# Convolved units of a delta-net mixer summed in one region of a PSUM bank, with due work bound in order

## The chip, the core and the metric

The kernel runs on one core of one Trainium2 chip. The metric is the device time of one execution in microseconds, where lower is better. A core has TensorE (matmuls, PE in the profile, its weight loads PEld), VectorE (DVE), ScalarE (ACT), GpSimd (POOL) and SyncE (SP), which issues most DMAs. Matmuls write to PSUM, which has eight banks of 128 partitions by 512 fp32 values; VectorE and ScalarE read it from there.

## What is computed

A decoder trunk of two layers over 256 tokens of width 1024. Each layer is a half SwiGLU feed-forward block, a token mixer, cross-attention into 256 memory tokens, and a second half feed-forward block. Layer 0 mixes by dilated window attention beside a gated linear recurrence; layer 1 by a gated delta net, whose q, k and v go through a causal convolution of four taps. Cut to the layers' frame and the second mixer:

```python
for layer in range(DEPTH):                                   # 2
    x = x + 0.5 * swiglu(rmsnorm(x, ffn1_norm[layer]), ffn1_w_in[layer], ffn1_w_out[layer])
    h = rmsnorm(x, mix_norm[layer])
    x = x + (attn_lru_mixer(h, ...) if layer % 2 == 0 else deltanet_mixer(h, ...))
    x = x + cross_attention(rmsnorm(x, xa_norm[layer]), rmsnorm(mem, xa_mem_norm[layer]), ...)
    x = x + 0.5 * swiglu(rmsnorm(x, ffn2_norm[layer]), ffn2_w_in[layer], ffn2_w_out[layer])
return rmsnorm(x, final_norm)

def deltanet_mixer(h, w_in, conv_w, a_log, dt_bias, o_norm, w_out):   # 8 heads of 128
    qkv, z, a, b = jnp.split(h @ w_in, [3 * W, 4 * W, 4 * W + DN_HEADS], axis=-1)
    qkv = jax.nn.silu(causal_dwconv(qkv, conv_w))
    q, k, v = jnp.split(qkv, 3, axis=-1)
    q, k = l2norm(q.reshape(shp)), l2norm(k.reshape(shp))
    beta = jax.nn.sigmoid(b)
    g = -jnp.exp(a_log) * jax.nn.softplus(a + dt_bias)
    o = gated_delta_rule_chunked(q, k, v, g, beta)
    o = rmsnorm(o, o_norm) * jax.nn.silu(z)
    return o.reshape(B, S, W) @ w_out
```

## The kernel before

Activations lie transposed: 128 partitions of features by 256 tokens, eight such pieces for the width of 1024. To keep fp32 accuracy with the fast fp32r products, every operand is split into a rounded high part and the rest, the low part. A weight tile of 512 rows by 256 columns comes by DMA (`raw`, five buffers), ScalarE writes its high part (L158) and VectorE its low part (L159) into `wt` (four buffers).

A *unit* is 1024 rows by 256 columns of one weight matrix: two halves `j` of 128 output features, each over eight steps `k`. The generator `unit` takes one bank of PSUM for each half. In `mm3` a step is two products: the high weights times the moving high and low part side by side (512 columns, L200) and the low weights times the high part (256 columns, L204). The bank then holds two regions whose sum is the result; `add` copies one on ScalarE (L270) and adds the other on VectorE (L271). `unit_t` is the same with tokens and features exchanged (L216, L220). `parts` (L242) makes three products of 256 columns that all sum in one region; `unit_split` uses it, both halves in one bank, and reads that bank once at the end.

A unit yields after every four steps, four times in all. At each yield the driver (`run` or `fill`) calls `tick`, which splits one weight tile ahead, runs one piece of `later`, counts time up by one and runs the *due* work: `after(n, fn)` notes work that is to be issued n ticks on. The second mixer is written as units in a given order (`DN_ORDER`) with everything else as due work: betas, decays, the decay rows that go out to DRAM and come back by GpSimd's DMA (`decay`, L1119, exponentials L1125), norms (`sums`), transposes, the key matrices, the block inverses. Two groups of two head pairs then run a back substitution (`back`, twelve yields), alternately, and after each yield as many pieces of the next units as `DN_FILL` says; its last two numbers stand ahead of the transposes of the gated output (`gated_T`, L1348 to L1350) of the second group, and what is left of the units runs after them, ahead of the output projection.

The units of q, k and v in the second mixer (`unit` within `mixer1`) hand each half to `conv`: the addition into `xn`, a scaled copy by tap 3 on ScalarE (L1071) and three multiply-adds with the other taps on VectorE (L1074, 72 in all: 24 halves). psw, the pool that the units of this mixer take banks from, has three banks; the small products use pss (three) and psf (two).

The order written in the program is not the order of issue. A scheduler at compile time keeps each engine's instructions in one fixed queue, and takes those first that it believes ready first; equal ones go in the program's order. The engines then work through their queues in order and wait on semaphores.

In the first mixer the heads run in a loop of ten rounds: scores of head h (`scores`), probabilities transposed for h - 1 (`weights`, L658), values for h - 2 (`values`, L892 to L894), then two pieces of other units.

## Time and profile before

| | us |
|---|---|
| median of three runs | 1252.77 |
| lowest and highest run | 1252.73, 1253.04 |
| the profiled execution | 1251.99 |
| its span (first to last instruction) | 1250.2 |
| TensorE busy | 1236.0 (99%) |
| VectorE busy | 929.0 (74%) |
| ScalarE busy | 752.0 (60%) |
| first mixer's attention rounds, from and to | about 252, 296 |
| second mixer's units, from and to | about 784, 949 |
| granted clock of TensorE | 0.998 |

All rows come from one profiled execution of the kernel. Times are from the start of its span. Matmuls overlap each other, and their ends are modelled, so the busy share of TensorE says little; what a product costs is read from its start to the next one's start. "idle" in a row is the time that the engine stood still just before, and the arrow names what ended it.

### The profile page before, as it was taken

The page shows a single profiled execution, that of the slowest core. Times are in us where ns is not written, and L with a number is a line of the kernel's source. Part 1 is how long each engine was busy: PE and PEld are TensorE (multiplying, and loading weights), DVE is VectorE, ACT ScalarE, POOL GpSimd, SP SyncE. Part 2 cuts the span into 40 slices and gives each one's busy share as a digit, 9 for nine tenths or more (in the row PEclk, how much of TensorE's full clock was granted, in tenths as well). Part 3 has the DMA queues.
Part 4 walks back from the last instruction along what each step waited for, and adds up shares of the span by engine and source line. Part 5 has one row for each costly group of instructions (what it writes and reads, how often), then busy time and mean ns, then how long its engine had stood idle before and what let it go on. Part 6 is the DMA issues. An engine that isn't in the chain of part 4 may idle for free.

```text
span 1250.2 us, 20300 instructions
## 1 busy us (share of the span) xinstructions
PE 1236.0 (99%) x7702; PEld 1104.9 (88%) x7702; DVE 929.0 (74%) x1590; ACT 752.0 (60%) x1281; POOL 80.5 (6%) x96
## 2 busy tenths in 40 slices
PE   9999999999999999999999999999999999999997
PEld 8888889888998888888888888888898998888887
DVE  6987957788668778766877756989757668777753
ACT  7766545886555665545656544776757465666543
POOL 1000020000101000011000001020001101000000
PEclk9999999999999999999999999999999999999999
DMA  8766676544544566557666566667534535666561
GB/s 272 215 206 197 185 255 185 178 125 152 185 135 154 185 198 184 183 185 231 187 187 195 181 192 204 183 153 193 142 99 135 181 124 169 185 186 194 177 194 60
DMA packets 231019, 222.92 MB, mean 178 GB/s; under 512 B 14969, under 2 KB 228617, under 8 KB 230793
## 3 DMA queue, kind: packets, MB, share of 16 engines
q1 hardware_dynamic: 229448, 217.94, 56.9%
q0 software_dynamic: 1152, 3.15, 1.0%
q8 instruction: 60, 0.98, 0.3%
q10 hardware_dynamic: 320, 0.53, 0.1%
q14 instruction: 39, 0.31, 0.1%
HBM read 215.03 MB, written 5.51 MB: 176 GB/s over the span
## 4 chain that ended last, share of the span: by engine, by line
PE 90%; DVE 5%; ACT 2%; DMA 1%; issue 1%; POOL 1%; ACTq 0%; DVEq 0%; POOLq 0%
PE psw L200 21%; PE pss L200 16%; PE psw L204 11%; PE psf L200 11%; PE pss L204 8%; PE psf L204 5%; PE psw L242 5%; PE psf L242 4%; PE pss L242 3%; PE psw L216 2%; DVE wt L159 1%; PE psw L220 1%; ACT wt L158 1%; PE pss L1268 1%; PE psf L1274 1%
## 5 line engine op out<-in xcount | busy, mean ns | idle before, releaser
L159 DVE TENSOR_TENSOR wt<-raw,wt 128x1024 fp32r<-128x1024 f32 (+1 forms) x409 | 484.9, 1191 | 202.8 <-ACT wt L158 199.6
L158 ACT ACTIVATE wt<-raw 128x1024 fp32r<-128x1024 f32 (+1 forms) x409 | 418.6, 1031 | 172.1 <-PE psw L204 59.4
L200 PE MATMUL psw<-x,wt 128*128 128x512 f32 x864 | 310.6, 396 | 2.1 <-DVE xn L271 1.8
L204 PE MATMUL psw<-x,wt 128*128 128x256 f32 x864 | 224.9, 281 | 0.5 <-DVE wt L159 0.5
L200 PE MATMUL pss<-x,wt 128*128 128x512 f32 x520 | 187.4, 393 | 0.0
L200 PEld LDWEIGHTS psw<-x,wt 128*128 128x128 f32 x864 | 160.6, 188 | 30.1 <-issue 2.1
L204 PEld LDWEIGHTS psw<-x,wt 128*128 128x128 f32 x864 | 162.4, 188 | 9.4 <-DVE wt L159 1.0
L204 PE MATMUL pss<-x,wt 128*128 128x256 f32 x520 | 134.9, 280 | 0.0
L200 PE MATMUL psf<-x,wt 128*128 128x512 f32 x352 | 127.2, 394 | 0.0
L200 PEld LDWEIGHTS pss<-x,wt 128*128 128x128 f32 x520 | 97.7, 188 | 16.9 <-ACT bc L377 0.4
L204 PEld LDWEIGHTS pss<-x,wt 128*128 128x128 f32 x520 | 97.7, 188 | 5.4
L200 PE MATMUL psw<-h,wt 128*128 128x512 f32 x264 | 94.9, 396 | 0.0
L204 PE MATMUL psf<-x,wt 128*128 128x256 f32 x352 | 91.3, 280 | 0.0
L200 PE MATMUL pss<-h,wt 128*128 128x512 f32 x242 | 87.0, 396 | 0.0
L336 POOL TENSOR_TENSOR acc<-acc,sq 128x256 f32<-128x256 f32 x49 | 43.7, 891 | 658.3 <-ACT sq L334 557.3
L200 PEld LDWEIGHTS psf<-x,wt 128*128 128x128 f32 x352 | 66.1, 188 | 11.2
L204 PE MATMUL psw<-h,wt 128*128 128x256 f32 x264 | 72.0, 280 | 0.0
L204 PEld LDWEIGHTS psf<-x,wt 128*128 128x128 f32 x352 | 66.2, 188 | 3.5
L204 PE MATMUL pss<-h,wt 128*128 128x256 f32 x242 | 66.0, 280 | 0.0
L200 PEld LDWEIGHTS psw<-h,wt 128*128 128x128 f32 x264 | 49.6, 188 | 10.8
L200 PE MATMUL psf<-h,wt 128*128 128x512 f32 x154 | 55.4, 397 | 0.0
L200 PEld LDWEIGHTS pss<-h,wt 128*128 128x128 f32 x242 | 45.5, 188 | 9.8
(377 smaller groups left out, 2109.2 us busy)
## 6 DMA issues: line engine op xcount, KB each, us to landing
raw<-in_ffn_w_in_dram SPq DMA_DIRECT2D x175, 512.0 KB, 3.6
raw<-in_ffn_w_out_dram SPq DMA_DIRECT2D x80, 512.0 KB, 3.6
raw<-in_xa_wkv_dram SPq DMA_DIRECT2D x32, 512.0 KB, 3.5
raw<-in_dn_w_in_dram SPq DMA_DIRECT2D x32, 512.0 KB, 4.6
raw<-in_ab_w_in_dram SPq DMA_DIRECT2D x20, 512.0 KB, 3.6
raw<-in_xa_wq_dram SPq DMA_DIRECT2D x16, 512.0 KB, 3.5
raw<-in_xa_wo_dram SPq DMA_DIRECT2D x16, 512.0 KB, 3.4
raw<-in_ffn_w_out_dram SPq DMA_DIRECT2D x16, 256.0 KB, 2.9
```

What stands on the lines that cost most here:

```text
L158: nc.scalar.activation(a, r, AF.Copy)
L159: nc.vector.tensor_sub(b, r, a.bitcast(F32))
L200: nc.tensor.matmul(out.rearrange("p a s -> p (a s)"), w[:, 0, cols], mov[:, k].rearrange("p a s -> p (a s)"), start=k == start, stop=k == ...
L204: nc.tensor.matmul(out[:, 0], w[:, 1, cols], mov[:, k, 0], start=False, stop=False)
L216: nc.tensor.matmul(out.rearrange("p a s -> p (a s)"), mov[:, k, 0, tok], w.rearrange("p a s -> p (a s)"), start=k == 0, stop=k == KD - 1)
L220: nc.tensor.matmul(out[:, 0], mov[:, k, 1, tok], w[:, 0], start=False, stop=False)
L242: self.nc.tensor.matmul(out, a[u], b[w], start=first and i == 0, stop=last and i == 2)
L336: (eng or nc.gpsimd).tensor_add(self.acc, self.acc, sq)
L1268: nc.tensor.matmul(py[:, i], na[:, i], tu[:, 0, i], start=True, stop=True)
L1274: nc.tensor.matmul(pp[:, i], yy[:, i], tu[:, 1, i], start=True, stop=True)
```

## The change

Three things are changed.

The twelve units of q, k and v in the second mixer go through a new generator, `unit_sum`: one bank for both halves, three products a step (`parts`) that sum up in one region of 256 columns, and `conv` gets that region itself and reads it from PSUM, four times. The addition into `xn` is gone there. (`lead` is never set.)

`Net.last` keeps the latest matmul of `mm3`, `mm3t` and `parts`, and the latest two instructions of a weight split. `behind` opens a context in which every instruction on the same engine as one of these is issued after it, in the engine's queue; nothing waits for its end. `tick` runs all due work in it, for TensorE, ScalarE and VectorE; the first mixer runs `weights` and `values` in it, for TensorE alone. There, one of the two pieces of each round moves from the end to between `scores` and `weights`.

The second row of `DN_FILL`, the counts of pieces in the second group, loses three: those after the second and the fifth yield, and one of the five ahead of the first gated transposes.

```diff
--- before.py
+++ after.py
@@ -26,7 +26,7 @@
 NEG = -1e30
 
 DN_ORDER = ('k0 k1 q0 q1 k2 v0 k3 v1 z0', '01|v3 z1 v2 q2', 'q3', '23|z2 z3 K2 K3')
-DN_FILL = ((1, 1, 1, 1, 1, 1, 1, 1, 1, 2, 2, 1), (1, 1, 1, 1, 1, 1, 1, 1, 1, 1, 1, 0, 5, 0))
+DN_FILL = ((1, 1, 1, 1, 1, 1, 1, 1, 1, 2, 2, 1), (1, 0, 1, 1, 0, 1, 1, 1, 1, 1, 1, 0, 4, 0))
 YB = 5
 EB, QB, VB = (4, 3, 3)
 TWICE = 'k0 k1 q0 q1'.split()
@@ -76,7 +76,7 @@
         self.n_load = self.n_half = self.n_take = 0
         self.later = deque()
         self.banks, self.n_bank = "w", 0
-        self.now, self.due = 0, []
+        self.now, self.due, self.last = 0, [], {}
 
 
 
@@ -155,8 +155,8 @@
         for u in range(0, n, step):
             us = slice(u, min(n, u + step))
             a, b, r = wt[:, us, 0, :cols], wt[:, us, 1, :cols], raw[:, us, :cols]
-            nc.scalar.activation(a, r, AF.Copy)
-            nc.vector.tensor_sub(b, r, a.bitcast(F32))
+            self.last["act"] = nc.scalar.activation(a, r, AF.Copy)
+            self.last["dve"] = nc.vector.tensor_sub(b, r, a.bitcast(F32))
         self.halves.setdefault(i, []).append(wt)
 
     def w(self, name, c0):
@@ -178,7 +178,15 @@
             self.later.popleft()()
         self.now += 1
         while self.due and self.due[0][0] <= self.now:
-            self.due.pop(0)[2]()
+            with self.behind():
+                self.due.pop(0)[2]()
+
+    def behind(self, engines=("pe", "act", "dve")):
+
+        stack = ExitStack()
+        for e in engines:
+            stack.enter_context(self.tc.issue_after(self.last[e].ins))
+        return stack
 
     def after(self, n, fn):
 
@@ -197,8 +205,9 @@
             w = wts[i // 4][:, i % 4]
 
             def high():
-                nc.tensor.matmul(out.rearrange("p a s -> p (a s)"), w[:, 0, cols], mov[:, k].rearrange("p a s -> p (a s)"),
-                                 start=k == start, stop=k == stop - 1)
+                self.last["pe"] = nc.tensor.matmul(out.rearrange("p a s -> p (a s)"), w[:, 0, cols],
+                                                   mov[:, k].rearrange("p a s -> p (a s)"),
+                                                   start=k == start, stop=k == stop - 1)
 
             def low():
                 nc.tensor.matmul(out[:, 0], w[:, 1, cols], mov[:, k, 0], start=False, stop=False)
@@ -213,8 +222,8 @@
             w = wts[k // 4][:, k % 4]
 
             def high():
-                nc.tensor.matmul(out.rearrange("p a s -> p (a s)"), mov[:, k, 0, tok], w.rearrange("p a s -> p (a s)"),
-                                 start=k == 0, stop=k == KD - 1)
+                self.last["pe"] = nc.tensor.matmul(out.rearrange("p a s -> p (a s)"), mov[:, k, 0, tok],
+                                                   w.rearrange("p a s -> p (a s)"), start=k == 0, stop=k == KD - 1)
 
             def low():
                 nc.tensor.matmul(out[:, 0], mov[:, k, 1, tok], w[:, 0], start=False, stop=False)
@@ -239,7 +248,7 @@
     def parts(self, out, a, b, first=True, last=True):
 
         for i, (u, w) in enumerate(((0, 0), (0, 1), (1, 0))):
-            self.nc.tensor.matmul(out, a[u], b[w], start=first and i == 0, stop=last and i == 2)
+            self.last["pe"] = self.nc.tensor.matmul(out, a[u], b[w], start=first and i == 0, stop=last and i == 2)
 
     def unit_split(self, name, c0, mov, dst, tokens=False):
 
@@ -254,6 +263,21 @@
             if j and ks.stop == KD:
                 self.split(dst, bank)
             yield
+
+    def unit_sum(self, name, c0, mov, take, lead=False):
+
+        wts = self.w(name, c0)
+        bank = self.bank_w()
+        sums = [bank[:, 0], self.bank_w()[:, 0] if lead else bank[:, 1]]
+        for j, ks in (LEAD if lead else STEADY):
+            js = slice(j * P, j * P + P)
+            for k in ks:
+                w = wts[k // 4][:, k % 4]
+                self.parts(sums[j], [w[:, i, js] for i in range(2)], [mov[:, k, i] for i in range(2)], k == 0, k == KD - 1)
+            if ks.stop == KD:
+                take(j, sums[j])
+            if len(ks) == 4 or j:
+                yield
 
     def unit_t(self, name, c0, mov, take):
 
@@ -950,14 +974,17 @@
             for h in range(10):
                 if h < 8:
                     sc[h] = scores(h)
+                self.fill(bg, 1)
                 if 1 <= h < 9:
-                    pts[h - 1] = weights(*sc.pop(h - 1))
+                    with self.behind(("pe",)):
+                        pts[h - 1] = weights(*sc.pop(h - 1))
                 if h >= 2:
                     i = h - 2
                     if i % 2 == 0:
                         po = self.bank("s")
-                    values(i, pts.pop(i), po)
-                self.fill(bg, 2)
+                    with self.behind(("pe",)):
+                        values(i, pts.pop(i), po)
+                self.fill(bg, 1)
             self.fill(bg)
             self.flush()
             self.project_out("ab_w_out", a2, gnext)
@@ -1063,10 +1090,8 @@
 
                 return mp.tile([P, 4, P], F32, name=name, bufs=bufs)
 
-            def conv(y, j, f, ps):
-
-                x = mp.tile([P, S], F32, name="xn", bufs=2)
-                self.add(x, ps)
+            def conv(y, j, f, x):
+
                 tap = lambda i: self.dcw[:, 24 * i + f:24 * i + f + 1]
                 nc.scalar.activation(y[:, j], x, AF.Copy, scale=tap(3))
                 for i in (2, 1, 0):
@@ -1365,8 +1390,8 @@
                     return
                 a = "qkv".index(kind)
                 y = mp.tile([P, 2, S], F32, name="y", bufs=YB)
-                yield from self.unit("dn_w_in", a * 1024 + c * 256, mov,
-                                     lambda j, ps: conv(y, j, a * 8 + 2 * c + j, ps))
+                yield from self.unit_sum("dn_w_in", a * 1024 + c * 256, mov,
+                                         lambda j, x: conv(y, j, a * 8 + 2 * c + j, x))
                 twice = 2 if step in TWICE else 1
                 silu(y, twice)
                 if kind == "k":
```

## Rows read from the trace of the kernel before

**Rows 1.** The page, part 1: busy us, share of span, instructions.
```profile
PE 1236.0 (99%) x7702; PEld 1104.9 (88%) x7702; DVE 929.0 (74%) x1590; ACT 752.0 (60%) x1281; POOL 80.5 (6%) x96
```

**Rows 2.** The page, part 4: shares of the chain that ended last.
```profile
PE 90%; DVE 5%; ACT 2%; DMA 1%; issue 1%; POOL 1%; ACTq 0%; DVEq 0%; POOLq 0%
```

**Rows 3.** Busy time by stretch of the second mixer: stretch, length, engines (instructions), clock, DMA.
```profile
784.00:845.00 61.00, 58.76 (x366) 51.71 (x365) 54.78 (x154) 46.88 (x95) 9.35 (x9) 1.00 0.67 166
...
902.00:949.00 47.00, 46.57 (x343) 43.49 (x344) 27.12 (x60) 30.42 (x74) 4.20 (x4) 1.00 0.25 80
```

**Rows 4.** TensorE's timeline: start, length, engine, line, operation, out<-in, count, [idle<-releaser].
```profile
818.39 0.39 PE L200 MATMUL psw<-x,wt 128*128 128x512 f32 x1
820.62 0.47 PE L200 MATMUL psw<-x,wt 128*128 128x512 f32 x1 [1.84 <-DVE xn L271]
...
843.75 0.47 PE L216 MATMUL psw<-wt,x 128*128 128x512 f32 x1 [0.40 <-DVE tm L1233]
...
845.70 0.50 PE L216 MATMUL psw<-wt,x 128*128 128x512 f32 x1 [0.29 <-DVE xn L271]
...
900.76 0.68 PE L1348 MATMUL pss<-ident,qk 128*128 128x128 f32 x3
902.43 0.33 PE L1348 MATMUL pss<-ident,qk 128*128 128x128 f32 x1 [1.00 <-DVE qk L1339]
...
951.97 0.28 PE L204 MATMUL psw<-a,wt 128*128 128x256 f32 x1
953.60 0.50 PE L200 MATMUL psf<-a,wt 128*128 128x512 f32 x1 [1.34 <-DVE a L1350]
```

**Rows 5.** TensorE's timeline in the first mixer.
```profile
290.31 0.98 PE L242 MATMUL psw<-m,wt 128*128 128x256 f32 x7
292.00 0.30 PE L658 MATMUL pss<-ident,pe 128*128 128x128 f32 x1 [0.70 <-DVE pe L656]
```

**Rows 6.** TensorE's timeline: the two forms of a step.
```profile
821.05 0.40 PE L200 MATMUL psw<-x,wt 128*128 128x512 f32 x1
...
821.75 0.39 PE L200 MATMUL psw<-x,wt 128*128 128x512 f32 x1
...
350.94 5.87 PE L242 MATMUL psf<-x,wt 128*128 128x256 f32 x48
356.65 1.59 PE L242 MATMUL pss<-kT,qT 128*128 128x256 f32 x12
```

**Rows 7.** Groups in 784 to 845: busy us, mean ns | idle before, releasers.
```profile
L1074 DVE SCALAR_TENSOR_TENSOR y<-xn,dcw,y 128x255 f32<-128x255 f32 (+2 forms) x42 | 19.8, 474 | 1.1 <-ACT y L1071 1.1
L159 DVE TENSOR_TENSOR wt<-raw,wt 128x1024 fp32r<-128x1024 f32 x16 | 19.5, 1219 | 0.6 <-ACT wt L158 0.5
L271 DVE TENSOR_TENSOR xn<-psw,xn 128x256 f32<-128x256 f32 x15 | 6.2, 414 | 0.1
...
L1071 ACT ACTIVATE y<-xn,dcw 128x256 f32<-128x256 f32 x14 | 7.1, 504 | 1.7 <-DVE xn L271 1.6
L270 ACT ACTIVATE xn<-psw 128x256 f32<-128x256 f32 x16 | 6.0, 373 | 2.5 <-PE psw L200 2.5
```

**Rows 8.** Groups of the whole span, columns as in rows 7.
```profile
L397 DVE SCALAR_TENSOR_TENSOR xT<-psw,xT 128x256 f32<-128x256 f32 x48 | 20.1, 419 | 5.2 <-PE psw L200 4.7
...
L1268 PEld LDWEIGHTS pss<-tu,na 128*128 128x128 f32 x96 | 11.3, 191 | 0.6 <-ACT tu L1281 0.2 <-DMA tu<-d 0.2
...
L1275 DVE COPY_PREDICATED tu<-dn_m,psf 128x512 f32<-128x512 uint8 x12 | 8.6, 731 | 3.4 <-PE psf L1274 3.4
...
L1280 PEld LDWEIGHTS pss<-ident,tu 128*128 128x128 f32 x32 | 3.7, 141 | 0.5 <-DVE tu L1275 0.3
...
L1307 ACT ACTIVATE q<-pss,eg 128x128 f32<-128x128 f32 x8 | 2.5, 368 | 3.8 <-DVE vb L1304 3.8
```

**Rows 9.** Timeline of ScalarE and of GpSimd.
```profile
817.51 0.99 ACT L1125 ACTIVATE e<-e,ngc 128x128 f32<-128x128 f32 x3 [3.95 <-DMA e<-gd]
...
811.35 3.66 POOL L1119 DMA_DIRECT2D e<-gd  x4 [0.81 <-DMA gd<-gt]
```

## The prediction

> **What bounds the kernel now.** I read the page first. TensorE is busy for 99% of the span [rows 1], and 90% of the chain that ended last is TensorE's own work [rows 2]. So nothing done on another engine is worth time by itself. A change can win only where TensorE stands still, or loses by making it stand still or by giving it more to stream. I then read the windows of the second mixer: in its first stretch VectorE is busy for 54.78 of 61 us, in the last one for 27.12 of 47 [rows 3]. The reader should see that VectorE is nearly full where eight convolved units follow each other, although TensorE still sets the pace.
>
> The third view is TensorE's timeline. Matmuls overlap, so a stall is read from start to start: a product of 512 columns is followed 0.23 us later by the next, one of 256 columns 0.12 us later, a small fp32 product 0.11 us later. Going through the second mixer by that rule, five stalls above 0.25 us belong to work that the diff touches [rows 4]: 818.39 to 820.62 is 2.23 us instead of 0.23, so 2.00 lost; the rows at 843.75 and 845.70 have 0.40 and 0.29 of idle time; the four transposes of a gated output should take 900.76 + 3 x 0.11 = 901.09, but the fourth starts at 902.43, 1.34 lost; 951.97 to 953.60 loses 1.51. The first three wait for L271, the addition that frees a bank of psw (or for small work queued ahead of it on VectorE); the fourth for the gating (L1339); the fifth for the last split of a gated output (L1350), which the output projection needs. In the first mixer one transpose of probabilities waits: seven products of 0.118 from 290.31 end at 291.14, and the next starts at 292.00, 0.86 lost [rows 5]. All this is 2.69 + 1.34 + 1.51 + 0.86 = 6.40 us. That is the whole prize.
>
> **The change part by part.** *Sums in one region.* For each of 12 units with a convolution the pair "512 columns, then 256" becomes three products of 256, each with its own weight load. Columns are the same, 768. From rows [rows 6]: two steps of the old form from 821.05 to 821.75, 0.35 us each; 48 products of the new form (16 steps) from 350.94 to 356.65, 0.119 each, 0.357 a step. 12 x 16 = 192 steps x 0.007 = **+1.3 us**, on TensorE, so on the path. Ends: +0.5 to +2, since a step's start is given to 0.01. The Trainium skill, "TensorE: Matmul & The Clock Gate", section "Back-to-back issue gap", has N / 2.4 + 2.5 ns, by which a third product would cost 2.5 ns a step; an estimate by that page is 0.5 us for all 192, and the rows' 0.231 us for 512 columns is longer than its 0.216.
>
> What goes is the addition: 24 copies on ScalarE of 0.37 us (L270) and 24 additions on VectorE of 0.41 (L271), of the 15 or 16 of each in the first stretch [rows 7]. On VectorE that is 15 x 0.41 = 6.2 of its 54.78 busy us there. The three taps (L1074, 0.474 each) and the scaled copy (L1071, 0.50) stay, but read PSUM; the nearest row, a SCALAR_TENSOR_TENSOR with a PSUM operand, is 0.419 against 0.474 from SBUF [rows 7, 8]. So the taps become no dearer; 0 to -0.06 each, off the path. I book nothing for relief by itself; it counts through the stalls below.
>
> *The bank waits (2.69 us).* A unit now needs one bank where it needed two, so the three banks of psw hold three units instead of one and a half, and the addition that the stalled products waited for is gone. Against it: the 2.00 us have a second cause. ScalarE stood 3.95 us for the decay rows that come by DMA (e<-gd), loaded by GpSimd from 811.35 on, and the exponentials held its queue [rows 9]. These loads and that landing stay; the softplus chain that leads to them shares VectorE with the additions and gets faster. Binding the due exponentials behind the last split doesn't move them if that split was done long before. I take **-2.2** of the 2.69; ends 0 and -2.69.
>
> *Due work bound behind products and splits.* On TensorE due products come after the tick's last product, on ScalarE and VectorE after the last split. Queued behind a bound instruction on VectorE or ScalarE are the taps of the next unit; behind a bound product, the next products. The masks, stores and loads of SP and GpSimd are not bound; only their producers move. No row of TensorE's waits in this mixer was ended by a weight split, so later stores ahead of weight loads on SP's queue are booked at nothing; were the five raw buffers used up, each load held back would cost its own delay. The gated transposes (1.34 us) are among the bound: they come behind the products of their tick, with gating done by then. GpSimd's power ahead of them is untouched. I take **-1.1**, ends 0 and -1.34.
>
> *The fill counts.* Three of sixteen pieces of z and K go from between the back-substitution steps and from ahead of the gated transposes to after them: the projection's wait of 1.51 gets three pieces of four steps, 3 x 4 x 0.35 = 4.2 us, as cover. What is next late: two steps (the counts that became 0) lose their piece and see the predicated copy of 0.73 us (L1275, [rows 8]) uncovered unless due products stand there; I leave 0.1 for it. **-1.4**; ends -1.51 and 0 (both holes open, 2 x 0.73).
>
> *First mixer.* A piece of four steps now lies between scores and weights, and the weights' transposes come behind it, so the 0.86 us get a cover of 1.4. **-0.7**; ends 0 and -0.86.
>
> *The new wait.* Both halves of a unit now lie in one bank. The first half's convolution reads while the second half's products want to write there. Does the program let them? In the back substitution ScalarE's L1307 reads columns of a bank that VectorE's L1304 does not touch and needs none of its results, and yet waits for it, 3.8 us in all [rows 8]. So readers of one bank are held apart whatever their columns, and I expect the same for TensorE: twelve locks. The Trainium skill, "PSUM — Partial Sum Buffer", section "PSUM bank collisions raise a hardware error", says that engines must be guarded by bank and quadrant, not by address; it speaks against this change, and the row of L1307 agrees. Bare, a lock lasts as long as the scaled copy and three taps, 0.50 + 3 x 0.474 = 1.92 us [rows 7], so 12 x 1.92 = 23 us if TensorE has nothing else. It has: the next unit's first half lies in another bank and is 8 x 0.35 = 2.8 us long, and due products come first. The nearest rows are the back-substitution steps, where TensorE also waits for an evacuation of its own result with other products in between: L1268 and L1280 lost 0.6 and 0.5 us in 24 and 8 groups of four, 0.03 to 0.06 a group [rows 8]. The convolution is longer than such an evacuation, so I take 0.1 each, **+1.2**; ends 0 (a wait can't give time) and +23.
>
> **Sum.** -2.2 - 1.1 - 1.4 - 0.7 + 1.3 + 1.2 = -2.9 us. The profiled execution took 1251.99 us, 1250.2 of it the span and 1.8 around it; with the change 1249.1. The median of the three runs is 1252.77, 0.78 above the profiled one, so the forecast is 1252.77 - 2.9 = about **1249.8**.
>
> **The rivals.** *The locks stay open (slower).* Where the next unit's weights are not split in time, or the convolution queues behind a split (1.2 us, L159 [rows 7]), the cover is too short. For it speaks that VectorE is 90% busy in the first stretch; against it that 6.2 us of that go. Without locks the sum is -4.1, so it turns at 4.1 / 12 = 0.34 us a lock. At half the bare price, 0.96 each or 11.5 in all, the time is 1252.77 - 4.1 + 11.5 = 1260; at 0.7 each it is 1257. This is also what the bank rule gives as a mechanism.
>
> *One wait takes the other's place (no change).* The exponentials still hold ScalarE's queue for the DMA, so the 2.00 us stay (they may now hold a convolution and with it a lock), and locks cost 0.2: -5.4 + 2.0 + 1.3 + 2.4 = +0.3, 1253.1. For it: the DMA chain isn't touched.
>
> *All stalls go.* Locks are wholly covered: -6.40 + 1.3 = -5.1, 1247.7. For it: the due work that fills a lock is now placed there by name. Against it: 818 us has the DMA behind it.
>
> **How the numbers follow.** Forecast 0.45 (three quarters of it below the line of "faster"), all stalls go 0.20, no change 0.18, locks open 0.17. About 0.2%, 2.5 us, is what a measurement of this kernel can tell from no change; faster is below 1250.3, slower above 1255.3. Faster 0.35 + 0.20 = 0.55; same 0.10 + 0.18 = 0.28; slower 0.17. The range reaches from 1246.0 (all stalls and a little more) to 1257.0 (locks of 0.7 us) and leaves out about 0.15. The likeliest case alone spans 1248 to 1251.5.
>
> **What the changed profile would show.** L271 on xn gone but for the one of the gates; 576 more products at the line of the three-product form in place of 192 at L200 and 192 at L204; TensorE's waits in the first stretch ended by L1074 (a lock), each under 0.2 us if I'm right, near 1 if the slower rival is; the stall near 952 gone and products of K between the last gated transposes and the projection; no wait of 1 us at L1348; the transposes of the first mixer behind a piece, without the 0.86. I'm wrong if waits ended by L1074 sum to over 4 us, if ScalarE's wait for e<-gd still stops TensorE for 2 us, or if the three-product step takes over 0.36 us.

## The result and the profile after

The change made the kernel slower: a median of 1263.68 us (1262.35 to 1264.69, five runs) against 1252.77 (1252.70 to 1255.92, five runs), a ratio of 1.0079 with a 95% interval of 1.0065 to 1.0093. That is 10.9 us more where 2.9 less was forecast, and above the range. The profiled execution took 1264.2 us, 1262.4 of it the span, so 12.2 us of span have to be found.

Runs of the kernel before and of several below spread by some 3 us along with TensorE's mean granted clock (last section), so each ratio is to the kernel before on the same chip in the same batch.

The page of the kernel after, part 1, answers [rows 1]:

```profile
PE 1243.2 (98%) x7894; PEld 1118.6 (89%) x7894; DVE 923.0 (73%) x1566; ACT 748.6 (59%) x1259; POOL 80.7 (6%) x96
```

192 more products, 24 fewer instructions on VectorE (the additions), 22 fewer on ScalarE (24 copies gone, two table loads more, of which below): the edit is in. The stretches of the second mixer (columns as in [rows 3]; the last three are shorter ones within the first, or just behind it):

```profile
784.00:845.00 61.00, 54.83 (x417) 52.50 (x416) 48.16 (x126) 41.10 (x77) 7.64 (x8) 0.93 0.60 157
902.00:949.00 47.00, 44.98 (x347) 41.92 (x346) 26.76 (x54) 30.05 (x74) 4.90 (x4) 1.00 0.33 102
800.00:815.00 15.00, 13.10 (x98) 12.68 (x97) 11.28 (x36) 9.02 (x19) 3.44 (x5) 0.89 0.43 112
830.00:845.00 15.00, 12.33 (x86) 11.57 (x85) 11.40 (x31) 12.93 (x23) 2.01 (x2) 0.84 0.45 112
845.00:860.00 15.00, 14.63 (x104) 13.57 (x104) 11.63 (x40) 8.07 (x15) 1.01 (x1) 0.93 0.48 126
```

In 784 to 845 TensorE is busy for 54.83 us where it was 58.76, and VectorE (48.16 from 54.78), ScalarE and GpSimd are less busy too. Nobody is full; they wait for each other. Something else is new: the granted clock is 0.93 in that stretch and was 1.00. It is at one of two levels, 1.00 (2.4 GHz) or 0.50 (1.2 GHz), so the three short rows hold (0.11 + 0.16 + 0.07) x 15 / 0.5 = 10.2 us at half clock, which cost up to 5.1.

What TensorE waited for from 784 on (engine, line <- what ended the wait: us in total, times, longest), with what ScalarE waited for in 784 to 860 before it could split weights, in the kernel after:

```profile
PE psw L251 <- DVE wt L159: 3.3, 4, 1.9
PE psw L251 <- ACT wt L158: 2.2, 1, 2.2
PE psw L251 <- DVE y L1099: 1.6, 1, 1.6
...
ACT wt L158 <- PE psw L251: 8.1, 5, 3.5
```

The same lines of the kernel before:

```profile
PE psw L200 <- DVE xn L271: 1.8, 1, 1.8
PE psf L200 <- DVE a L1350: 1.3, 1, 1.3
PE pss L1348 <- DVE qk L1339: 1.0, 1, 1.0
...
ACT wt L158 <- PE psw L204: 3.7, 4, 1.2
```

The waits that the change aimed at are gone or small. In their place stand 5.5 us ended by a *weight split* (L158, L159), of which the kernel before had none, and 1.6 us ended by a tap of the convolution (L1099), the lock proper. Worked out from the starts of neighbouring products in 784 to 966, the time above each shape's usual pitch (0.231 us for 512 columns, 0.117 for 256) was 8.4 us before and is 20.6 after: 12.2 more, as much as the span grew. 5.3 us of it lie in the stretches at half clock (a wait of 0.47 us among them); the rest, some 7, is above all stalls.

**How the lock reaches the splits.** The second half of a unit cannot start while the first half's convolution reads its bank, so the scheduler puts the next unit's first half in between. The order of issue on TensorE in the program of the kernel after (buffers numbered, due products left out; a weight tile gives 12 products to each half):

```
L251 MATMUL psw_8157<-x2_79,wt_8076 x12      first half of a unit
L251 MATMUL psw_8157<-x2_79,wt_8106 x12
L251 MATMUL psw_8255<-x2_79,wt_8170 x12      first half of the next one
L251 MATMUL psw_8255<-x2_79,wt_8191 x12
L251 MATMUL psw_8157<-x2_79,wt_8076 x12      second half of the first
L251 MATMUL psw_8157<-x2_79,wt_8106 x12
L251 MATMUL psw_8255<-x2_79,wt_8170 x12      second half of the next one
L251 MATMUL psw_8255<-x2_79,wt_8191 x12
```

Two units hold all four `wt` buffers; the first comes free after the fifth line. From then it is 12 + 24 = 36 products, 36 x 0.118 = 4.2 us, until the tile that takes its place is needed, and all four come free within that time. In the kernel before both halves of a unit followed each other, and a tile had a quarter of a unit and a whole one, 20 steps of 0.35 or 7.0 us. A split takes 1.05 us on ScalarE and then 1.22 on VectorE, and VectorE has for each two units 4 x 1.22 + 12 x 0.476 (taps) = 10.6 us of work in 96 x 0.118 = 11.3. There is hardly any slack for a late start. The kernel before had still more for VectorE, four additions of 0.41 us for each two units, and no wait for a split: it is the 4.2 us in place of 7.0 that is new.

TensorE's timeline of the kernel after shows the two largest stalls and what follows them (start, length, line, operation, count, [idle before <- releaser]):

```profile
802.66 0.95 PE L251 MATMUL psw<-x,wt 128*128 128x256 f32 x6
805.52 1.47 PE L251 MATMUL psw<-x,wt 128*128 128x256 f32 x7 [1.90 <-DVE wt L159]
...
810.34 0.95 PE L1128 MATMUL pss<-ones,th 128*128 128x1 f32 x8
...
837.11 0.85 PE L251 MATMUL psw<-x,wt 128*128 128x256 f32 x5
840.15 0.79 PE L251 MATMUL psw<-x,wt 128*128 128x256 f32 x2 [2.20 <-ACT wt L158]
841.41 5.76 PE L251 MATMUL psw<-x,wt 128*128 128x256 f32 x24 [0.47 <-DVE wt L159]
847.01 0.95 PE L1128 MATMUL pss<-ones,th 128*128 128x1 f32 x8
...
916.22 3.09 PE L251 MATMUL psw<-x,wt 128*128 128x256 f32 x24 [1.60 <-DVE y L1099]
```

Both stalls are ended by a split, and after both the clock is at half: the 24 products from 841.41 take 847.01 - 841.41 = 5.60 us, 0.233 each where 0.118 is usual. The last row is the one lock that TensorE met bare.

The split that ends the first stall, and the due work that stood behind the stall, in the timelines of ScalarE and VectorE:

```profile
799.39 1.05 ACT L158 ACTIVATE wt<-raw 128x1024 fp32r<-128x1024 f32 x1
...
802.38 0.63 ACT L1122 ACTIVATE th<-y 128x512 f32<-128x512 f32 x1 [0.33 <-DVE y L1106]
...
804.25 1.22 DVE L159 TENSOR_TENSOR wt<-raw,wt 128x1024 fp32r<-128x1024 f32 x1
```

ScalarE's half of the split was done at 800.44, but VectorE, busy all the while with taps, another split and due work, came to its own half 3.8 us later. The sums of squares (L1128) are due work. Their squares were ready at 803.01, and yet they stand *behind* the stall, at 810.34.

### The profile page after: what moved, and what is told of

Its sections match the earlier page's. It is cut to its first block, busy times and chain, and to the rows that moved or that the text cites. A ratio compares the mean times of both kernels' runs of the same rounds, so it can differ in the third digit from the quotient of the medians.

```text
span 1262.4 us, 20653 instructions
## 1 busy us (share of the span) xinstructions
PE 1243.2 (98%) x7894; PEld 1118.6 (89%) x7894; DVE 923.0 (73%) x1566; ACT 748.6 (59%) x1259; POOL 80.7 (6%) x96
## 4 chain that ended last, share of the span: by engine, by line
PE 86%; DVE 4%; issue 4%; DMA 3%; ACT 2%; POOL 1%; SPq 1%; ACTq 0%; POOLq 0%; DVEq 0%
PE psw L208 18%; PE pss L208 15%; PE psf L208 10%; PE psw L213 9%; PE pss L213 8%; PE psw L251 8%; PE psf L213 5%; PE psf L251 3%; PE pss L251 2%; DVE wt L159 1%; PE psw L225 1%; DMA raw<-in_ffn_w_in_dram 1%; PE pss L1293 1%; PE psf L1299 1%; ACT wt L158 1%
## 5 line engine op out<-in xcount | busy, mean ns | idle before, releaser
L159 DVE TENSOR_TENSOR wt<-raw,wt 128x1024 fp32r<-128x1024 f32 (+1 forms) x409 | 484.7, 1190 | 210.9 <-ACT wt L158 207.7
L158 ACT ACTIVATE wt<-raw 128x1024 fp32r<-128x1024 f32 (+1 forms) x409 | 418.3, 1030 | 186.1 <-PE psw L213 55.3
L208 PE MATMUL psw<-x,wt 128*128 128x512 f32 x680 | 245.7, 396 | 0.3 <-DVE x L335 0.2
L208 PE MATMUL pss<-x,wt 128*128 128x512 f32 x528 | 190.4, 393 | 0.0
L213 PE MATMUL psw<-x,wt 128*128 128x256 f32 x680 | 176.7, 280 | 0.8 <-DVE wt L159 0.8
L208 PEld LDWEIGHTS psw<-x,wt 128*128 128x128 f32 x680 | 127.1, 188 | 22.8 <-DVE x L335 0.8
L213 PEld LDWEIGHTS psw<-x,wt 128*128 128x128 f32 x680 | 127.8, 188 | 8.3 <-DVE wt L159 1.4
L208 PE MATMUL psf<-x,wt 128*128 128x512 f32 x336 | 121.3, 393 | 0.0
L251 PE MATMUL psw<-x,wt 128*128 128x256 f32 x816 | 109.9, 291 | 7.6 <-DVE wt L159 3.3
L251 PEld LDWEIGHTS psw<-x,wt 128*128 128x128 f32 x816 | 103.0, 195 | 10.1 <-DVE wt L159 4.2
L213 PE MATMUL psf<-x,wt 128*128 128x256 f32 x336 | 87.2, 280 | 0.0
L208 PE MATMUL psw<-h,wt 128*128 128x512 f32 x242 | 86.9, 396 | 0.0
L208 PEld LDWEIGHTS psf<-x,wt 128*128 128x128 f32 x336 | 63.1, 188 | 10.7
L213 PEld LDWEIGHTS psf<-x,wt 128*128 128x128 f32 x336 | 63.1, 188 | 3.4
L213 PE MATMUL psw<-h,wt 128*128 128x256 f32 x242 | 66.0, 280 | 0.0
L208 PE MATMUL psf<-h,wt 128*128 128x512 f32 x176 | 63.2, 396 | 0.0
```

The costliest lines, as they stand in the source:

```text
L158: self.last["act"] = nc.scalar.activation(a, r, AF.Copy)
L159: self.last["dve"] = nc.vector.tensor_sub(b, r, a.bitcast(F32))
L208: self.last["pe"] = nc.tensor.matmul(out.rearrange("p a s -> p (a s)"), w[:, 0, cols], mov[:, k].rearrange("p a s -> p (a s)"), start=k == ...
L213: nc.tensor.matmul(out[:, 0], w[:, 1, cols], mov[:, k, 0], start=False, stop=False)
L251: self.last["pe"] = self.nc.tensor.matmul(out, a[u], b[w], start=first and i == 0, stop=last and i == 2)
```

## The experiments

**The lock and the rest, apart.** First theory: the shared bank alone does it. Second: the lock is covered, and the bound due work does it. `two_banks` gives each half its own bank and leaves the rest of the change in:

```diff
         bank = self.bank_w()
-        sums = [bank[:, 0], self.bank_w()[:, 0] if lead else bank[:, 1]]
+        sums = [bank[:, 0], self.bank_w()[:, 0]]
```

> The changed kernel, but each half of a convolved unit sums up in a bank of its own, so that the second half's products need not wait for the first half's convolution. Everything else of the change stays. Theory of the lock (one bank for both halves holds the second half back, two units' weight tiles stay held, splits come late, and TensorE's clock falls after the longest of these stalls): most of the 10.9 us go, 1250 to 1255, no stretch at half clock in the second mixer, no wait of TensorE over 1 us that a weight split ends. Theory of the binding (due work behind products and splits delays what others need): little changes, 1261 to 1265. Theory of the form (three products and three weight loads a step are dearer than the two): 1261 to 1265 as well.

Measured: 1252.49 us against 1252.85, ratio 0.9988 (0.9971 to 1.0005). The whole loss is gone, with binding, three-product steps, fill counts and first mixer as in the kernel after. In its profile the split waits are 0.3 us, the clock in the second mixer is 1.00, and in its order of issue the two halves of a unit follow each other again. So the loss needs the lock; it's the bank, not the region, that is locked.

`sum_only` is the kernel before with the generator `unit_sum` and the convolution from the bank, and nothing else of the change:

```diff
-            def conv(y, j, f, ps):
+            def conv(y, j, f, x):
...
-                x = mp.tile([P, S], F32, name="xn", bufs=2)
-                self.add(x, ps)
...
-                yield from self.unit("dn_w_in", a * 1024 + c * 256, mov,
+                yield from self.unit_sum("dn_w_in", a * 1024 + c * 256, mov,
```

> The kernel before with the new units alone: one bank, three products a step, convolution read from the bank; no binding, old fill counts, old order in the first mixer. Theory of the lock: as slow as the whole change, 1259 to 1270, since nothing else makes it slow. Theory of the binding: near 1252. Theory of the form: 1254 at least, by the 1.3 us of the steps, with no stall that the kernel before doesn't have.

`no_sum` is the other part: the kernel after with the old `unit` and the old `conv`.

```diff
-            def conv(y, j, f, x):
+            def conv(y, j, f, ps):
...
+                x = mp.tile([P, S], F32, name="xn", bufs=2)
+                self.add(x, ps)
...
-                yield from self.unit_sum("dn_w_in", a * 1024 + c * 256, mov,
+                yield from self.unit("dn_w_in", a * 1024 + c * 256, mov,
```

> The changed kernel with the units of q, k and v as they were before (two banks, two regions, addition into xn); binding, fill counts and the first mixer's order stay changed. Theory of the lock: about the kernel before or a little faster, 1248 to 1254. Theory of the binding: slower than before by several us, 1258 to 1265. Theory of the form: 1248 to 1254.

Measured: `sum_only` 1256.28, ratio 1.0023 (1.0013 to 1.0033), and `no_sum` 1255.81, ratio 1.0016 (1.0003 to 1.0029). By these medians the lock alone costs 3.4 us and the rest alone 3.0; together they cost 10.9. At least some 4 us belong to neither part, so they work on each other. (The rest alone may be worth less: the profile of `no_sum` has no wait for a split, but 6.9 us at half clock, up to 3.4 us of time, behind the old stall of [rows 4]; the last section has more on this.) `sum_only` has the same kind of split waits, in its view of waits from 784 to 860:

```profile
ACT wt L158 <- PE psw L242: 10.0, 5, 3.8
...
PE psw L242 <- DVE wt L159: 1.0, 2, 0.8
PE psw L216 <- DVE wt L159: 1.0, 1, 1.0
```

ScalarE waits even longer for a free tile than in the kernel after, yet TensorE waits 2.0 us for splits and not 5.5. What makes the splits dear is the other part.

`short_lock` shortens the lock: ScalarE copies the region once, and the convolution reads the copy.

```diff
-            def conv(y, j, f, x):
+            def conv(y, j, f, ps):
 
+                x = mp.tile([P, S], F32, name="xn", bufs=2)
+                nc.scalar.activation(x, ps, AF.Copy)
```

> The changed kernel, but one ScalarE copy takes the region out of the bank into xn and the convolution reads that, so that the second half waits for one copy of about 0.37 us in place of a scaled copy and three multiply-adds (0.47 and 3 x 0.48). Both halves still share a bank. Theory of the lock: its length decides, so most of the loss goes, 1251 to 1257, against which 24 more copies stand on ScalarE. Theories of the binding and of the form: 1261 to 1265.

Measured: 1256.01, ratio 1.0014 (1.0001 to 1.0027), with one copy of 0.38 us in place of a scaled copy and three taps. Most of the loss goes, so its length matters. Not all of it goes: the halves of two units still alternate in its order of issue, and its profile has waits of 2.05 and 0.75 us for splits near 819.

**Which binding.** `no_bind` runs the due work in `tick` unbound; the lock stays.

```diff
         while self.due and self.due[0][0] <= self.now:
-            with self.behind():
-                self.due.pop(0)[2]()
+            self.due.pop(0)[2]()
```

> The changed kernel with the due work unbound again: units in one bank, new fill counts and the first mixer's new order stay. The units alone cost 3.4 us and the rest without them 3.0 in the runs so far, while both together cost 10.9. Theory that lock and binding make each other worse (due work no longer fills the time in which the second half waits, or waits itself behind a split that has no free tile): 1254 to 1257, at most what the units alone cost. Theory that the costs just add and the excess is the clock that falls after long stalls: 1257 to 1261.

`bind_pe` and `bind_actdve` bind on TensorE alone, and on ScalarE and VectorE alone:

```diff
-            with self.behind():
+            with self.behind(("pe",)):
```

> The changed kernel with due work bound on TensorE alone. If TensorE's lost fillers are what makes the lock dear: 1260 to 1265, with a wait of about 2 us ended by a weight split or a tap. If it is due work held on ScalarE and VectorE behind splits that wait for a free tile: 1254 to 1258.

```diff
-            with self.behind():
+            with self.behind(("act", "dve")):
```

> The changed kernel with due work bound on ScalarE and VectorE alone. The mirror of the run with TensorE alone: 1254 to 1258 if TensorE's fillers count, 1260 to 1265 if the held queues of ScalarE and VectorE do.

Measured: `no_bind` 1255.26, ratio 1.0005 (0.9985 to 1.0025); `bind_pe` 1262.17, ratio 1.0056 (1.0037 to 1.0074); `bind_actdve` 1257.78, ratio 1.0021 (1.0005 to 1.0037). With the lock in place, binding on TensorE costs 1.0056 - 1.0005 = 0.5%, some 6 us, and on the other two 0.16%, 2 us, which is within the intervals. TensorE's timeline of `no_bind`, at the same place as the stall at 805.52 (its lines are one lower):

```profile
803.06 0.83 PE L250 MATMUL psw<-x,wt 128*128 128x256 f32 x5
803.95 0.28 PE L1082 MATMUL pss<-ident,gch 128*16 128x128 f32 x1
804.07 1.01 PE L1127 MATMUL pss<-ones,th 128*128 128x1 f32 x8
805.70 0.44 PE L1177 MATMUL psf<-ident,y 128*128 128x128 f32 x2 [0.63 <-DVE y L1105]
```

The due sums (L1127) run in the hole, and 0.63 us of it is left where 1.90 were; what TensorE waits for there is no split. In `bind_pe` the hole is back:

```profile
807.36 1.10 PE L251 MATMUL psw<-x,wt 128*128 128x256 f32 x7 [1.89 <-DVE wt L159]
...
810.63 0.95 PE L1128 MATMUL pss<-ones,th 128*128 128x1 f32 x8
```

Bound behind the tick's last product, a due product can't pass a product that waits for its weights. The binding forbids this filling. And there is a second effect: the same split as above, ScalarE's and VectorE's half in `no_bind`:

```profile
797.88 1.05 ACT L158 ACTIVATE wt<-raw 128x1024 fp32r<-128x1024 f32 x1
...
800.07 1.23 DVE L159 TENSOR_TENSOR wt<-raw,wt 128x1024 fp32r<-128x1024 f32 x1
```

VectorE comes to it 1.1 us after ScalarE is done, where it was 3.8 in the kernel after; in `bind_pe` it is 3.8 again, in `bind_actdve` and `sum_only` 1.2. So with due work bound on TensorE the order on VectorE, which isn't bound in `bind_pe`, is also one in which this split comes late. Which of the two effects costs more isn't shown.

What binding on ScalarE does is seen in its timeline of the kernel after:

```profile
831.66 1.85 ACT L1150 ACTIVATE e<-e,ngc 128x128 f32<-128x128 f32 x6
833.53 1.28 ACT L1108 ACT_TABLE_LOAD   x1
834.82 0.63 ACT L1108 ACTIVATE y<-y 128x512 f32<-128x512 f32 x1
835.47 1.28 ACT L1150 ACT_TABLE_LOAD   x1
836.77 0.40 ACT L1150 ACTIVATE e<-e,ngc 128x128 f32<-128x128 f32 x1
...
839.05 1.05 ACT L158 ACTIVATE wt<-raw 128x1024 fp32r<-128x1024 f32 x1
```

A Silu (L1108) has come between the exponentials (L1150), and each change between these two loads a table, 1.28 us. A third load follows at 841.83. From 784 to 960 the kernel after loads four, `bind_actdve` four, and every other kernel here two (`two_banks`, `late_take` and `short_lock` are bound on ScalarE as well, so it takes the lock's order, too). The split at 839.05 is the one that ends the stall of 2.20 us at 840.15; two extra loads, 2.6 us, stand in ScalarE's queue ahead of it.

`two_banks_no_bind` takes out both causes, by the diffs of `two_banks` and `no_bind` together:

```diff
-            with self.behind():
-                self.due.pop(0)[2]()
+            self.due.pop(0)[2]()
...
-        sums = [bank[:, 0], self.bank_w()[:, 0] if lead else bank[:, 1]]
+        sums = [bank[:, 0], self.bank_w()[:, 0]]
```

> Two banks a unit, three products a step, convolution from the bank, new fill counts, first mixer's new order, and due work unbound. With the lock gone binding should matter little: 1250 to 1255, within 2 us of the run with two banks and binding (1252.5). If binding is a gain by itself once the lock is away, this one is slower than that by more than 1.5 us.

Measured: 1251.04 against 1253.54, ratio 0.9976 (0.9957 to 0.9995). Without the lock, binding costs 0.12%, 1.5 us, which is within the intervals; with it 1.0079 - 1.0005 = 0.74%, 9 us.

**One bank without a lock.** `late_take` keeps both halves in one bank and has both convolutions read after the second half's last product, so nobody reads while products are to come:

```diff
-            if ks.stop == KD:
-                take(j, sums[j])
+            if j and ks.stop == KD:
+                for i in range(2):
+                    take(i, sums[i])
```

> The changed kernel with one thing moved: both halves still sum up in one bank, but both convolutions are issued after the second half's last product, so that no product waits for a reader of its bank. Binding, fill counts, three products a step and reading from the bank stay. If the lock on the second half is the cause: 1250 to 1255, no wait on a weight split over 1 us in the second mixer. If holding one bank for long, reading it four times or the binding by itself were: 1259 to 1265.

`late_take_no_bind` is the same with the due work unbound:

```diff
-            with self.behind():
-                self.due.pop(0)[2]()
+            self.due.pop(0)[2]()
...
-            if ks.stop == KD:
-                take(j, sums[j])
+            if j and ks.stop == KD:
+                for i in range(2):
+                    take(i, sums[i])
```

> The same with the due work unbound. With two banks unbinding gave 1.4 us less (1251.0 against 1252.5 within their intervals); if binding only takes freedom from the order, 1249 to 1253 here and not slower than the bound one by more than 1 us.

Measured: `late_take` 1252.82 against 1254.14, ratio 0.9995 (0.9984 to 1.0007); `late_take_no_bind` 1250.87, ratio 0.9975 (0.9964 to 0.9985), faster than both kernels. So sharing a bank costs nothing; reading one half while the other is due does. From `late_take_no_bind`: the stretch 784 to 845, TensorE's waits from 784 on, and ScalarE's wait for tiles (784 to 860).

```profile
784.00:845.00 61.00, 60.79 (x505) 59.91 (x506) 54.42 (x151) 43.96 (x86) 9.71 (x9) 1.00 0.70 184
```

```profile
PE pss L1373 <- DVE qk L1364: 1.3, 2, 0.9
PE pss L1293 <- DMA tu<-d: 1.0, 2, 0.6
...
ACT wt L158 <- PE psw L250: 10.5, 7, 2.8
```

TensorE is busy for 60.79 of 61 us. ScalarE waits 10.5 us for free tiles here, longer than in the kernel after, and no product waits for a split. In `late_take`, with due work bound, it waits 10.3 us, and again no product waits for a split. So a long wait for a free tile is harmless by itself. In the order of issue of `late_take` the two halves of a unit follow each other again, so that a split has the longer time.

**The two small parts.** `fill_only` is the kernel before with the new counts, and `two_banks_no_bind_old_m0` is `two_banks_no_bind` with the loop of the first mixer as before:

```diff
-DN_FILL = (..., (1, 1, 1, 1, 1, 1, 1, 1, 1, 1, 1, 0, 5, 0))
+DN_FILL = (..., (1, 0, 1, 1, 0, 1, 1, 1, 1, 1, 1, 0, 4, 0))
```

> The kernel before with the new fill counts alone. The prediction's step for them: 1.4 us less, since three pieces then stand between the last gated transposes and the projection, which waited 1.51 us: 1251 to 1252, the wait on L1350 gone. If the two emptied places open by as much: 1252.5 to 1253.5.

```diff
-                self.fill(bg, 1)
                 if 1 <= h < 9:
-                    with self.behind(("pe",)):
-                        pts[h - 1] = weights(*sc.pop(h - 1))
+                    pts[h - 1] = weights(*sc.pop(h - 1))
...
-                    with self.behind(("pe",)):
-                        values(i, pts.pop(i), po)
-                self.fill(bg, 1)
+                    values(i, pts.pop(i), po)
+                self.fill(bg, 2)
```

> Two banks, unbound, new fill counts, and the first mixer as it was before, against the same with the first mixer's new order (1251.0). The prediction's step: the new order is worth 0.7 us, so 1251 to 1252.5 here. By the traces the 0.86 us wait went but three smaller ones of 0.34 to 0.56 stand in its place, so that nothing was won: 1250 to 1251.2.

Measured: `fill_only` 1255.18 against 1254.14, ratio 1.0006 (0.9995 to 1.0018). The wait of the output projection (L1350), 1.3 us, is gone, but the gated transposes wait longer (1.4 us in two, from 1.0 in one) and two steps of the back substitution now wait 0.4 (L1274) and 0.3 us (L1280). Its profile also has a stretch at half clock, behind a stall that lies before the first changed count, for which see the last section. `two_banks_no_bind_old_m0`: 1252.42, ratio 0.9981 (0.9967 to 0.9994), beside 0.9976 with the new loop. The two can't be told apart.

## Why the prediction was wrong

**What bounds the kernel: right.** Time went where TensorE stood still or its clock was low, and nowhere else.

**Three-product steps, +1.3: right.** In `late_take_no_bind` 76 such products run on end:

```profile
790.05 9.16 PE L250 MATMUL psw<-x,wt 128*128 128x256 f32 x76
```

The next product starts at 799.42 after 0.21 of idle time. Pitch is (9.16 - 0.28) / 75 = 0.118 us, with 0.28 for the last one's own length; 0.355 a step, 192 x 0.005 = +1.0. Taps from PSUM take 0.476 us where 0.474 was, as said.

**Bank waits, -2.2: the mechanism was right, and hidden.** No product waits for an addition of these units any more. The wait of ScalarE for the decay rows, 4.0 us in [rows 9], is 1.8 in the kernel after and is not seen in `late_take`, but it is 3.4 in `two_banks`, so the decay rows are not always earlier. A gain shows once the lock and the binding are away: `late_take_no_bind` at 0.9975 is 3.1 us below before, where the sum without the lock's +1.2 was -4.1. That the two are near is partly luck. Three terms of that sum were wrong (below), and many runs of the kernel before lose time at half clock (last section). The profiled executions, of which neither has such a fall in the mixer, have spans of 1249.0 and 1250.2: 1.2 us, which is what -2.2 and +1.0 give, as far as one execution of each can tell.

**The new wait, +1.2: the step that failed.** I priced a lock by the groups of the back substitution, at 0.1 us, with the next unit's first half and due products as cover. Waits ended by a tap are indeed only 1.6 us in all, one of them; by my own test (over 4 us) I would have been right, though that one wait was to be under 0.2. But both covers had a price that I didn't work out. The next unit's first half takes that unit's two weight tiles while the first unit still holds its own, and so all four buffers: the lock was paid at L158 and L159, not at L1099. And due products could not come first, since the same change binds them behind the products that wait. I had said that no wait of TensorE was ended by a split, and booked the binding on that: in the kernel before it was so, and the change takes it away. The sum had +1.2 for locks and -1.1 for the binding; `no_bind` against the kernel after shows that with the lock the binding costs 9 us. The rival named late splits as the place where a lock stays open, and took 1257 to 1260; it was the right case, and still too small. What it left out is the half clock, up to 5.1 us, for which no term stood in any sum. One lock proper and five waits for splits are 7.1 us of idle time, some 0.6 a lock where 0.1 was booked.

The Trainium skill's rule, which the prediction held against the change, is to guard PSUM by bank and quadrant and not by address ("PSUM — Partial Sum Buffer", section "PSUM bank collisions raise a hardware error"). The traces agree: products into one half of a bank wait for the taps that read its other half (1.60 us at 916.22), and with a bank for each half the ratio goes from 1.0079 to 0.9988.

**Binding, -1.1: wrong.** The gated transposes wait 0.4 us after and 1.0 before, but 1.4 in `no_sum` and 1.3 in `late_take`, which are bound, too, and 0.4 in `two_banks_no_bind`, which isn't. The order of issue around them changes with each kernel; the binding isn't the reason. What binding does do is cost 1.5 to 2.5 us without the lock (`two_banks`, `late_take` against their unbound versions) and 9 with it.

**Fill counts, -1.4: wrong.** The projection's wait went, as said, but no time came of it. Steps of the back substitution and the transposes wait instead, 0.4 + 0.3 + 0.4 = 1.1 us for the 1.3; I had left 0.1 for it. By the interval of `fill_only` a gain above 0.6 us is left out, though most of its runs have the lower mean clock, which the counts don't explain (last section).

**First mixer, -0.7: wrong.** The 0.70 us of idle time in [rows 5] became three waits that sum to more (view of waits, 252 to 300, kernel after):

```profile
PE pss L682 <- DVE pe L680: 0.9, 3, 0.4
```

The one hole became three smaller ones; in `two_banks_no_bind` they are 0.8 us in three, with the old loop 0.6 in one. That the moved piece is now missing at its old place would explain it, and is argued, not shown.

**Still open.** Of the 12.2 us that the second mixer lost, 5.3 lie in the stretches at half clock. Nearly as much can be lost with less of it: `bind_pe`, whose span is 11.7 us above before, has 3.4 us at half clock, up to 1.7 us of time. What decides when the clock falls stays open (last section), and so does which of the two effects of binding on TensorE weighs more. Whether more weight buffers would take the sting out of the lock wasn't tried.

## What to carry to other kernels

Two results in one bank make a lock as soon as one is read before the other is finished; read them after the last product, or give each a bank. Before a wait is called covered, list what the covering work holds (buffers, tiles, queue places) and who is next for it: the bill may come at another line. Binding low-priority work behind the main stream keeps it out of the way, and out of the holes as well; on ScalarE it can also put two functions in turns, a table load for each.

## What the runs showed of the hardware

In the kernel after, TensorE's clock fell to half right after stalls of 1.9 and 2.2 us at 805.52 and 840.15, for (0.11 x 15) / 0.5 = 3.3 and (0.16 + 0.07) x 15 / 0.5 = 6.9 us. I had not expected a stall of this size to cost twice. It isn't certain to: the kernel before kept 1.00 after its 1.84 us [rows 3, 4], `short_lock` after 2.05, and `bind_pe` after the 1.89 us at 807.36 shown above. `fill_only`, whose order of issue on TensorE is that of the kernel before until after 857 us, has the old stall, 2.01 us at 820.47, and a fall right behind it (its stretch 815 to 830):

```profile
815.00:830.00 15.00, 12.99 (x65) 11.59 (x64) 11.49 (x31) 11.96 (x32) 2.18 (x2) 0.77 0.87 195
```

It has the same clock of 0.77 in this stretch as `no_sum`, whose stall there is 2.13 us. Nor does it take a stall of 2 us. In `sum_only` the clock falls behind eight products of one column and a wait of 0.64 us (timeline, then the stretch 800 to 815):

```profile
804.93 1.01 PE L1116 MATMUL pss<-ones,th 128*128 128x1 f32 x8
806.57 0.44 PE L1166 MATMUL psf<-ident,y 128*128 128x128 f32 x2 [0.64 <-DVE y L1094]
...
800.00:815.00 15.00, 14.32 (x108) 13.87 (x107) 11.69 (x34) 9.77 (x22) 4.74 (x6) 0.89 0.67 154
```

In `bind_pe` it falls at 826 behind waits of 0.46 and 0.54 us, and in `bind_actdve` at 836 behind 0.43 and 0.36 (0.77 in 830 to 845). So the length of one wait doesn't tell whether the clock falls.

The fall seems to be behind the spread of the times: of 31 runs of the kernel before beside `two_banks`, 20 took 1251.3 to 1253.8 us at a mean clock of 0.998 to 1.000, and 11 took 1255.0 us or more at 0.997 or less; of the ten of `fill_only` eight took 1254.9 us or more at 0.997 or less. In all ten of `late_take_no_bind`, whose longest wait in the mixer is 0.9 us, the clock is 0.999 or more and the time 1249.7 to 1252.5. That the fall is what divides the runs is argued, from `fill_only` above all, as no run of the kernel before was profiled with it. When it falls after such a stall and when not, the runs don't show.
